# Queries of seven heads by seven block products, the third output block summed in its bank, output rows turned two blocks at a time

## The chip, the cores and the metric

The kernel runs on one core of one Trainium2 chip. The metric is the device time of one execution in microseconds (us). Three runs of the kernel before were timed, and one further execution was profiled. Engine names are those of the profile: PE does matmuls (PEld is its weight load), DVE and ACT are the two elementwise engines, POOL does a few tiny operations, SP issues most transfers. One core means no contention with other cores.

## The reference

Two layers over 528 positions (16 learned ones ahead of 512 tokens) of width 1024, in float32. The first is gated linear attention with four heads; the second is differential attention with eight heads, and this is where two of the three edits lie. Cut to the second layer:

```python
proj = xn @ w_in                       # (528 x 1024) @ (1024 x 8192)
q, k, v, z = jnp.split(proj, 4, axis=-1)          # 2048 columns each: 8 heads x 256
for each head, each block of 128 queries:
    s = einsum('qd,kd->qk', q, k) * 128 ** -0.5 + bias     # two score maps per head
    p = softmax(where(causal, s, -inf))
    a = p[0] - lam * p[1]
    o = head_rms(a @ v) * gnorm * (1 - lambda_init)        # 128 x 256
y = silu(z) * o
out = y @ w_out                                   # (528 x 2048) @ (2048 x 1024)
h = h + out;  final rmsnorm
```

## The kernel before

**Precision.** Every float32 operand is held as a high and a low part (tags ending in h and l, or a pair of tiles): `split` writes the high part by an ACT copy and the low part by a DVE subtraction. A product of two operands is then three matmuls: high by high, high by low, low by high.

**Units.** Most projections of 256 columns are a `Unit`. The 1024 x 256 weights are taken as 2 x 2 blocks of 512 x 128 and the normalised input as 2 x 2 blocks (inner half by token half), and the four output blocks come from seven block products p1 to p7 instead of eight (the Winograd scheme). One product is 12 matmuls (`PASSES`: 4 steps of 128 rows x 3) of 264 columns, or of 256 where only real tokens are wanted (z in the second layer). The scheme needs sums of weight blocks on DVE (`sums` and `outer` in `want_unit`, 4 additions of 128 x 512) and splits of three single blocks (a11, a12, a22: 128 x 512 each) and of two pairs (s21, s43: 128 x 1024 each). The input's own sums are made once per layer.

A unit's bank `bx` runs: p1 is summed in it and copied out by ACT as u1 (`partial`, line 452), p6 is added and copied as u2, p7 is added and copied as u3. The outputs are (0,0) = p1 copy and p2 in bank `by`; (0,1) = u2 and p5 + p3 in bank `bv`; (1,1) = u3 and p5 in `bv`; the third block (1,0) = u3 and p4. In the kernel before, p4 has a bank of its own (`by`, or the second `bx`), and a DVE operation joins it with u3 (line 477). Where a further unit is next in the queue, its p1 is issued between p7 and p4; where none is, p2 or other work stands there. `bx` has two buffers, `by` and `bv` one each.

**Queries.** Head 0's queries, and in the kernel before all heads' queries, are a plain projection (`project`, line 421): two output blocks, each 24 matmuls of 512 columns into one bank, whose result `split` takes from the bank with the scale (lines 279 and 280).

**Order of the work.** The instructions of PE are in program order, which a `Weaver` sets: the attention steps of one head (A scores, B turn the weights, C values, E rows: turn the output, multiply by the gate, split) are issued one after another, and between two steps so many microseconds of queued projection work are filled in (`W.fill`, with an estimated cost per piece). Per head the queue holds z, v, k and q of the next head, in heads 2, 4 and 6 with the output product of two earlier heads ahead of them. k may not start before the last scores of the head are issued (`W.stop`), so k and q stand beside the later steps; before the next head's first scores the queue is worked off and 3.0 us of the following work are filled in. ACT, DVE, POOL and SP are ordered by a scheduler with priorities (`at_once` above `urgent` above `soon`) and run in that order. Weights arrive in `raw` (two buffers) by transfers issued on SP, and are prepared ahead of use as far as buffers allow.

Of the kernel before, what the change touches and what calls it, by code (L numbers as in the profile page):

```python
# [209 lines left out]
def trunk(ctx, tc, x, meta, g_norm, gla_w_in, gla_w_gate_up, gla_b_gate, gla_gnorm, gla_w_out,  # L210
# [225 lines left out]
    class Unit:  # L436
# [26 lines left out]
        def run(self):  # L463
# [4 lines left out]
            nxt = nxt if isinstance(nxt, Unit) else None  # L468
            out = []

            @at_once
            def add(i, n, bank, t, sign):
                if not out:
                    out.extend(o if isinstance(o, list) else [o[:, :self.n], o[:, self.n:]] for o in self.dst())
                o, bank = out[i][n], bank[:, :self.n]
                if sign < 0:
                    W.mark = dve.scalar_tensor_tensor(o, bank, -sc, t, op0=ALU.mult, op1=ALU.subtract)
# [9 lines left out]
                add(0, 0, by, self.p1, 1)  # L487

            def p4():
                bz = pb_tile("by" if nxt else "bx")  # L490
                yield from product(bz, ws.use(a22), X["t4"])
                ws.done(a22)
                add(1, 0, bz, self.u3, -1)
                self.tail(1)

            def p5():
# [937 lines left out]
    def normed():  # L1434
# [11 lines left out]
        spare.update({(2304,): (0, 1, 2), (0, 8, 256): (3,)})  # L1446

# [18 lines left out]
    def want_diff(c):  # L1466
        ws.want_in_order((d_w_in, 0, KT, c), halves_of(P))
# [95 lines left out]
    def tok_tile():  # L1563
        return T(ep, [P, 2 * (256 + NM)], F32, "t", bufs=3)
# [83 lines left out]
        return W.add(gen(), 10.3)  # L1648

    def q_diff_q(hd, s):  # L1650
        want_diff(256 * hd)

        def gen():
            for i in range(2):
                bank = pb_tile("bx" if hd else ("bv", "by")[i])
                yield from project(ws.take(), real2, None, NR, [by_halves(bank)])
                assert not hd or heads[hd - 1].scored
                if i == 0:
                    s.q = [T(ep, [P, 2, NR], F32R, f"q{j}", bufs=1) for j in range(2)]
                urgent(split)(*[t[:, i, :] for t in s.q], bank, scale=-float(P) ** -0.5)  # L1660
        return W.add(gen(), 10.3)

    def diff_steps(hd, s, ys):
# [55 lines left out]
            act.activation(r.on, po, AF.Copy, scale=ms)  # L1719

        @urgent
        def rows(r):
            pt = ps_tile()
            for m in range(2):
                pe.transpose(pt[:, m * P:(m + 1) * P], r.on[:, m * P:(m + 1) * P], ident)  # L1725
            y = T(ep, [P, 2, P], F32, "yt")
            cs = slice(r.ta, r.ta + P)
            W.mark = dve.tensor_tensor(y, pt[:, :256].rearrange("p (m c) -> p m c", m=2), s.z[:, :, cs], op=ALU.mult)
            split(ys[hd][0][:, :, cs], ys[hd][1][:, :, cs], y)

        R = {}
# [1 line left out]
        def A(b):  # L1733
            R[b] = scores(b)

        return A, lambda b: turn(R[b]), lambda b: values(R[b]), lambda b: rows(R[b])

    def want_last(hd):

# [95 lines left out]
    for hd in range(D_HEADS):  # L1835
# [20 lines left out]
        if hd == D_HEADS - 2:  # L1856
# [3 lines left out]
            def freed():  # L1860
# [7 lines left out]
        share = {A: 1.5, B: 1.1, C: 1.1, E: 0.5}  # L1868
        if last:
            steps = steps[:6]  # L1870
        W.fill(3.0)
# [80 lines left out]
```

## Time and profile before

| | |
|---|---|
| median of three runs | 972.04 us (972.03 to 972.95) |
| span of the profiled execution, first to last instruction | 970.2 us, 1.84 us under the median of the runs; the page gives no other time for that execution |
| granted PE clock, mean | 0.999 |
| first layer | to about 480 us |
| scores of the eight heads of the second layer begin at | 500.1, 552.3, 604.9, 678.7, 731.9, 805.3, 858.5, 913.1 us |
| DMA | 104.94 MB, 108 GB/s mean |

In the profile, "xN" is a count, and a group's row gives its busy time, the mean duration of one in ns, and the idle time of its engine just before it with what ended it. Durations of neighbouring instructions overlap, on PE strongly (a matmul's listed duration is two to three times its pace), so the pace of a run of matmuls is read from the start of one group to the start of the next.

### The profile page before, as it was taken

The page shows a single profiled execution, that of the slowest core. Times are in us where ns is not written, and L with a number is a line of the kernel's source. Part 1 is how long each engine was busy: PE and PEld are TensorE (multiplying, and loading weights), DVE is VectorE, ACT ScalarE, POOL GpSimd, SP SyncE. Part 2 cuts the span into 40 slices and gives each one's busy share as a digit, 9 for nine tenths or more (in the row PEclk, how much of TensorE's full clock was granted, in tenths as well). Part 3 has the DMA queues.
Part 4 walks back from the last instruction along what each step waited for, and adds up shares of the span by engine and source line. Part 5 has one row for each costly group of instructions (what it writes and reads, how often), then busy time and mean ns, then how long its engine had stood idle before and what let it go on. Part 6 is the DMA issues. An engine that isn't in the chain of part 4 may idle for free. (4 is left out here: it accounts for less than half of the span.)

```text
span 970.2 us, 18065 instructions
## 1 busy us (share of the span) xinstructions
PE 957.1 (99%) x6993; PEld 906.5 (93%) x6993; DVE 778.4 (80%) x1586; ACT 628.0 (65%) x1304; POOL 50.6 (5%) x68
## 2 busy tenths in 40 slices
PE   8999999999999999999999999999999999999997
PEld 8999999999999999898899998898998999989996
DVE  7989885886888887568997985977958879677785
ACT  7776755577647567656757774576764677655583
POOL 1000000000000100000001001001010000000001
PEclk9999999999999999999999999999999999999999
DMA  7322223635363245224355525135252352412212
GB/s 197 88 86 60 79 81 122 148 99 129 120 156 96 79 121 154 62 92 151 100 132 147 131 78 153 51 97 140 86 148 88 99 138 86 148 61 84 87 66 87
DMA packets 128521, 104.94 MB, mean 108 GB/s; under 512 B 51101, under 2 KB 112829, under 8 KB 128432
## 3 DMA queue, kind: packets, MB, share of 16 engines
q1 hardware_dynamic: 123104, 93.80, 35.1%
q10 hardware_dynamic: 5328, 9.95, 2.8%
q8 instruction: 56, 0.92, 0.4%
q14 instruction: 33, 0.27, 0.1%
HBM read 83.64 MB, written 11.80 MB: 98 GB/s over the span
## 5 line engine op out<-in xcount | busy, mean ns | idle before, releaser
L277 DVE TENSOR_TENSOR wl<-raw,wh 128x1024 fp32r<-128x1024 f32 x98 | 119.5, 1222 | 24.8 <-ACT wh L276 16.8
L276 ACT ACTIVATE wh<-raw 128x1024 fp32r<-128x1024 f32 x98 | 103.2, 1055 | 52.6 <-PE by L968 23.2
L431 PE MATMUL bv<-x,wh 128*128 128x264 f32 (+1 forms) x656 | 97.6, 286 | 0.0
L431 PE MATMUL bx<-x,wh 128*128 128x264 f32 (+1 forms) x640 | 94.9, 286 | 0.7 <-ACT u L452 0.6
L431 PEld LDWEIGHTS bv<-x,wh 128*128 128x128 f32 x656 | 86.5, 188 | 0.6 <-DVE z L479 0.3
L431 PEld LDWEIGHTS bx<-x,wh 128*128 128x128 f32 x640 | 84.5, 188 | 1.9 <-ACT u L452 1.2
L452 ACT ACTIVATE u<-bx 128x264 f32<-128x264 f32 (+1 forms) x120 | 45.4, 380 | 32.3 <-PE bx L431 31.1
L421 PE MATMUL bx<-x,wh 128*128 128x512 f32 (+1 forms) x256 | 62.4, 386 | 0.0
L277 DVE TENSOR_TENSOR wl<-sum,wh 128x1024 fp32r<-128x1024 f32 x41 | 50.1, 1221 | 14.3 <-ACT wh L276 13.9
L431 PE MATMUL bv<-x,wl 128*128 128x264 f32 (+1 forms) x328 | 55.2, 285 | 0.1
L1718 POOL TENSOR_TENSOR st<-st,mhalf 128x1 f32<-128x1 f32 x32 | 31.0, 970 | 464.4 <-ACT on L1716 408.9
L431 PE MATMUL bx<-x,wl 128*128 128x264 f32 (+1 forms) x320 | 53.9, 285 | 0.0
L1682 ACT ACTIVATE p<-p,st 128x528 f32<-128x528 f32 (+3 forms) x64 | 36.5, 571 | 25.4 <-DVE st L1680 24.9
L421 PEld LDWEIGHTS bx<-x,wh 128*128 128x128 f32 x256 | 44.5, 188 | 7.9
L276 ACT ACTIVATE wh<-sum 128x1024 fp32r<-128x1024 f32 x41 | 43.3, 1056 | 13.0 <-PE bv L431 4.0
L431 PE MATMUL by<-x,a12h 128*128 128x264 f32 (+1 forms) x320 | 46.5, 285 | 0.2 <-ACT t L1646 0.2
L431 PE MATMUL bx<-x,a11h 128*128 128x264 f32 (+1 forms) x320 | 46.3, 285 | 0.0
L431 PEld LDWEIGHTS bv<-x,wl 128*128 128x128 f32 x328 | 45.9, 188 | 0.4 <-issue 0.3
L431 PEld LDWEIGHTS bx<-x,wl 128*128 128x128 f32 x320 | 45.2, 188 | 0.6 <-DVE wl L277 0.2
L276 ACT ACTIVATE a11h<-raw 128x512 fp32r<-128x512 f32 x41 | 25.7, 627 | 28.6 <-DMA raw<-in_diff_w_in_dram 14.2
L431 PEld LDWEIGHTS bx<-x,a11h 128*128 128x128 f32 x320 | 42.2, 188 | 0.7
L431 PEld LDWEIGHTS by<-x,a12h 128*128 128x128 f32 x320 | 41.8, 188 | 0.4 <-ACT t L1646 0.4
(475 smaller groups left out, 2632.2 us busy)
## 6 DMA issues: line engine op xcount, KB each, us to landing
raw<-in_gla_w_in_dram SPq DMA_DIRECT2D x48, 512.0 KB, 4.5
raw<-in_diff_w_in_dram SPq DMA_DIRECT2D x42, 512.0 KB, 4.8
raw<-in_diff_w_in_dram SPq DMA_DIRECT2D x11, 1024.0 KB, 6.3
raw<-in_gla_w_out_dram SPq DMA_DIRECT2D x8, 1024.0 KB, 5.7
raw<-in_diff_w_out_dram SPq DMA_DIRECT2D x8, 1024.0 KB, 6.4
vd<-planes ACTq DMA_DIRECT2D x12, 268.0 KB, 7.1
vd<-keep ACTq DMA_DIRECT2D x12, 264.0 KB, 2.3
T<-bdr SPq DMA_DIRECT2D x8, 264.0 KB, 5.0
```

Source lines behind the costliest of these rows:

```text
L276: act.activation(hi, src, AF.Copy)
L277: dve.tensor_tensor(lo, src, hi.bitcast(F32), op=ALU.subtract)
L421: pe.matmul(bank, a[:, k, :], b[k] if n0 is None else b[k][:, n0 + i * nn:n0 + (i + 1) * nn], start=n == 0 and ks[0] == 0, stop=n == len(t ...
L431: pe.matmul(bank[:, :x[q].shape[2]], w[p][:, k * P:(k + 1) * P], x[q][:, k, :], start=first and i == 0, stop=i == len(PASSES) - 1, skip_gr ...
L452: W.moved = act.activation(t, self.bx[:, :self.n], AF.Copy, scale=self.sc)
L1682: act.activation(p[:, :nk], p[:, :nk], AF.Exp, scale=-1.0, bias=st[:, m:m + 1], accum_out=st[:, 2 + m:3 + m])
L1718: pool.tensor_tensor(ms, ms, mhalf[:, :1], op=ALU.pow)
```

## The change

1. **Queries of heads 1 to 7** are a `Unit` over the real tokens (256 columns per matmul), with the scale handed in; its results go to two SBUF tiles (`tok_tile`), and the split takes them from there instead of from the bank. Its cost estimate is 8.9 instead of 10.3 us. The transfer of one 1 MB weight tile becomes two of 512 KB.
2. **In every unit** (20 in the first layer, 21 in the second and the 7 new ones) p4 is added into `bx` after u3 has been copied, and the third block leaves the bank by an ACT copy with scale (`empty`, line 478 after) instead of the DVE operation.
3. **Rows of two blocks at once** in heads 0 to 6: step E is called twice per head instead of four times, with four transposes into one bank, one multiplication of 128 x 512 and one split of that size. Head 7 is as before.

```diff
             def p4():
-                bz = pb_tile("by" if nxt else "bx")
-                yield from product(bz, ws.use(a22), X["t4"])
+                yield from product(self.bx, ws.use(a22), X["t4"], False)
                 ws.done(a22)
-                add(1, 0, bz, self.u3, -1)
+                empty(1, 0)
                 self.tail(1)
+            @at_once
+            def empty(i, n):
+                act.activation(place(i, n), self.bx[:, :self.n], AF.Copy, scale=-sc)
...
     def q_diff_q(hd, s):
-        want_diff(256 * hd)
+        scale, qts = -float(P) ** -0.5, []
...
+        if hd:
+            def dst():
+                tiles()
+                qts.extend([tok_tile()[:, :NR], tok_tile()[:, :NR]])
+                return qts
+            @soon
+            def tail(i):
+                split(*[t[:, i, :] for t in s.q], qts[i])
+            return W.add(Unit(want_unit(d_w_in, 256 * hd), Xr, scale, dst, tail), 8.9)
...
-        def rows(r):
+        def rows(*rs):
+            w = P * len(rs)
             pt = ps_tile()
             for m in range(2):
-                pe.transpose(pt[:, m * P:(m + 1) * P], r.on[:, m * P:(m + 1) * P], ident)
-            y = T(ep, [P, 2, P], F32, "yt")
+                for j, r in enumerate(rs):
+                    pe.transpose(pt[:, m * w + j * P:m * w + (j + 1) * P], r.on[:, m * P:(m + 1) * P], ident)
+            y = T(ep, [P, 2, w], F32, "yt", bufs=1)
...
-        steps = [(A, 0), (A, 1), (B, 0), (A, 2), (C, 0), (B, 1), (E, 0), (A, 3), (C, 1), (B, 2), (E, 1), (C, 2), (B, 3),
-                 (E, 2), (C, 3), (E, 3)]
+        steps = [(A, 0), (A, 1), (B, 0), (A, 2), (C, 0), (B, 1), (A, 3), (C, 1), (B, 2), (E, 1), (C, 2), (B, 3),
+                 (C, 3), (E, 3)]
```

**Where instructions stand now.** The first place is p4 of a z unit in the second layer, on PE. `bx_9865` (before) and `bx_9899` (after) is the next unit's bank, with its p1; the rows that follow are p4. Before:

```order
L431 MATMUL bx_9865<-x_1512_8554,a11h_9736 128x264
L431 MATMUL bx_9865<-x_1513_8555,a11h_9736 128x264
L431 MATMUL bx_9865<-x_1512_8554,a11l_9737 128x264 x4
L431 MATMUL by_9880<-x_1543_8786,a22h_9714 128x256 x8
L431 MATMUL by_9880<-x_1543_8786,a22l_9715 128x256 x4
```

The same place after:

```order
L431 MATMUL bx_9899<-x_1492_8534,a11h_9770 128x264
L431 MATMUL bx_9899<-x_1493_8535,a11h_9770 128x264
L431 MATMUL bx_9899<-x_1492_8534,a11l_9771 128x264 x4
L431 MATMUL bx_9755<-x_1523_8766,a22h_9748 128x256 x8
L431 MATMUL bx_9755<-x_1523_8766,a22l_9749 128x256 x4
```

The products stand in the same order; p4 goes into this unit's own `bx_9755`, which ACT reads as u3 after p7, with one product of 12 matmuls between.

The second place is ACT at the end of head 1, where the queries of head 2 are finished (`q_1835`, after `q_1825`, is the high part of the queries; `wh` a weight pair, `hT` the rows of step E, `on` step C). Before:

```order
L276 ACTIVATE hT_8779<-yt_10343 128x2x128
L279 ACTIVATE q_1835_10360<-bx_10293 128x512
L1715 ACTIVATE ps_10350<-st_10121 128x1
L1716 ACTIVATE on_10355,st_10121<-ps_10350 128x257
L1719 ACTIVATE on_10355<-ps_10350,st_10121 128x256
L276 ACTIVATE wh_10414<-raw_10402 128x1024
L276 ACTIVATE hT_8779<-yt_10383 128x2x128
L279 ACTIVATE q_1835_10360<-bx_10364 128x512
```

The same place after:

```order
L1741 ACTIVATE on_10400<-ps_10395,st_10129 128x256
L452 ACTIVATE u_10426<-bx_10285 128x256
L276 ACTIVATE hT_8759<-yt_10448 128x2x256
L478 ACTIVATE t_10431<-bx_10285 128x256
L276 ACTIVATE q_1825_10428<-t_10431 128x512
L276 ACTIVATE wh_10502<-raw_10490 128x1024
L276 ACTIVATE q_1825_10428<-t_10430 128x512
```

The copy of u3 and the copy of the third block (line 478) are new here, the split reads tiles in SBUF, and one wide `hT` stands for two.

The third place is DVE at the same point: the last operations ahead of head 2's first scores (`wl` is the low part of a weight pair, `yt` step E's multiplication). Before:

```order
L1728 TENSOR_TENSOR yt_10343<-ps_10340,z_9193 128x256
L277 TENSOR_TENSOR wl_10411<-raw_10402,wh_10410 128x1024
L277 TENSOR_TENSOR hT_8779<-yt_10343,hT_8779 128x2x128
L280 SCALAR_TENSOR_TENSOR q_1836_10361<-bx_10293,q_1835_10360 128x512
L1728 TENSOR_TENSOR yt_10383<-ps_10380,z_9193 128x256
L277 TENSOR_TENSOR hT_8779<-yt_10383,hT_8779 128x2x128
L277 TENSOR_TENSOR wl_10415<-raw_10402,wh_10414 128x1024
L280 SCALAR_TENSOR_TENSOR q_1836_10361<-bx_10364,q_1835_10360 128x512
```

The same place after:

```order
L277 TENSOR_TENSOR wl_10499<-raw_10490,wh_10498 128x1024
L484 SCALAR_TENSOR_TENSOR t_10431<-bv_10391,u_10426 128x256
L1752 TENSOR_TENSOR yt_10448<-ps_10443,z_9172 128x512
L488 SCALAR_TENSOR_TENSOR t_10430<-by_10433,u_10307 128x256
L277 TENSOR_TENSOR hT_8759<-yt_10448,hT_8759 128x2x256
L277 TENSOR_TENSOR q_1826_10429<-t_10431,q_1825_10428 128x512
L488 SCALAR_TENSOR_TENSOR t_10430<-bv_10391,u_10389 128x256
L277 TENSOR_TENSOR wl_10503<-raw_10490,wh_10502 128x1024
L277 TENSOR_TENSOR q_1826_10429<-t_10430,q_1825_10428 128x512
```

Behind the last product of the query unit there are now a join (line 488), the ACT copy and the subtraction, where there were the ACT copy and the subtraction, and a `wl` of 1024 columns stands between join and subtraction.

More of the change, by code (lines that the diff above doesn't have):

```diff
@@ L469, in run, with place @@
             out = []
+            def place(i, n):
+                if not out:
+                    out.extend(o if isinstance(o, list) else [o[:, :self.n], o[:, self.n:]] for o in self.dst())
+                return out[i][n]
+            @at_once
+            def empty(i, n):
+                act.activation(place(i, n), self.bx[:, :self.n], AF.Copy, scale=-sc)
             @at_once
             def add(i, n, bank, t, sign):
-                if not out:
-                    out.extend(o if isinstance(o, list) else [o[:, :self.n], o[:, self.n:]] for o in self.dst())
-                o, bank = out[i][n], bank[:, :self.n]
+                o, bank = place(i, n), bank[:, :self.n]
                 if sign < 0:
@@ L1445, in normed @@
             W.defer(2.4 * i, lambda i=i: normed_pair(2 * i))
-        spare.update({(2304,): (0, 1, 2), (0, 8, 256): (3,)})
+        spare.update({(2304,): (0, 1, 2), (256,): (3,)})
     def halved(t):
@@ L1734, in A @@
             R[b] = scores(b)
-        return A, lambda b: turn(R[b]), lambda b: values(R[b]), lambda b: rows(R[b])
+        return A, lambda b: turn(R[b]), lambda b: values(R[b]), lambda b: rows(*([R[b]] if hd == D_HEADS - 1 else [R[b], R[b + 1]]))
     def want_last(hd):
```

17 lines of the change are left out of this document (10 added, 7 removed).

## Prediction

> **What bounds the kernel now.** I read the page's busy shares first, then the heads of the second layer by stage, then PE's timeline where a query projection ends and a unit begins, and last who waits for the copies out of the running bank.
>
> ```profile
> span 970.2 us, 18065 instructions
> PE 957.1 (99%) x6993; PEld 906.5 (93%) x6993; DVE 778.4 (80%) x1586; ACT 628.0 (65%) x1304; POOL 50.6 (5%) x68
> ```
>
> PE is without work for 970.2 - 957.1 = 13.1 us in all. A busy PE is not PE at its peak, though, so what is to be seen next is its pace. Two stretches of the timeline (start, length, engine, line, tiles, shape, count):
>
> ```profile
> 799.85 2.02 PE L421 MATMUL bx<-x,wl 128*128 128x512 f32 x8
> ...
> 801.71 1.11 PE L431 MATMUL bx<-x,a11h 128*128 128x256 f32 x8
> 802.66 0.64 PE L431 MATMUL bx<-x,a11l 128*128 128x256 f32 x4
> 803.13 1.11 PE L431 MATMUL by<-x,a12h 128*128 128x256 f32 x8
> ...
> 805.25 1.64 PE L400 MATMUL ps<-k,q 128*128 128x264 f32 x12
> ...
> 903.26 2.97 PE L421 MATMUL bx<-x,wh 128*128 128x512 f32 x12
> 906.06 0.38 PE L1725 MATMUL ps<-ident,on 128*128 128x128 f32 x2
> ...
> 909.07 1.14 PE L431 MATMUL bx<-x,a11h 128*128 128x264 f32 x8
> ...
> 910.53 1.14 PE L431 MATMUL by<-x,a12h 128*128 128x264 f32 x8
> ```
>
> Start to start: 8 query matmuls of 512 columns take 801.71 - 799.85 = 1.86 us, 0.2325 each (12 of them 2.80 us at 903.26, 0.2333 each). A product of 12 with 256 columns takes 803.13 - 801.71 = 1.42 us, 0.1183 each; one of 12 with 264 columns 910.53 - 909.07 = 1.46 us. The groups follow each other without a gap: the second layer lasts as long as PE's matmuls at their own pace. So an edit is worth what it takes off PE's list, less what it adds in waits.
>
> Whether DVE and ACT have room is read by stage (busy us and count of PE, PEld, DVE, ACT, POOL; then clock and DMA):
>
> ```profile
> 100.00:200.00 100.00, 100.00 (x792) 97.24 (x792) 80.47 (x159) 58.68 (x110) 3.50 (x5) 1.00 0.37 100
> ...
> 552.30:562.00 9.70, 9.70 (x80) 9.69 (x79) 9.60 (x26) 6.77 (x17) 0.00 (x0) 1.00 0.27 91
> 562.00:572.00 10.00, 10.00 (x85) 10.00 (x84) 9.78 (x25) 7.93 (x19) 1.37 (x1) 1.00 0.22 55
> 572.00:582.00 10.00, 10.00 (x85) 9.99 (x84) 6.34 (x19) 8.12 (x19) 0.81 (x1) 1.00 0.41 133
> 582.00:592.00 10.00, 10.00 (x72) 9.27 (x71) 6.64 (x15) 5.74 (x17) 2.02 (x2) 1.00 0.90 190
> 592.00:604.90 12.90, 12.90 (x63) 10.58 (x62) 5.84 (x10) 5.64 (x13) 0.65 (x1) 1.00 0.28 97
> ```
>
> The first row is in the first layer: DVE at 80%, PE never idle. The others are one head. In its first 19.7 us (z, v) DVE is 98% busy and PE does not lose anything, since weights are made ahead. In the last 32.9 us (k, q) DVE is busy 18.82 us and ACT 19.50 us. That is where the queries' extra work goes.
>
> **The queries.** Removed per head: 48 matmuls x 0.2325 = 11.16 us of PE. Added: 7 products of 12, 84 x 0.1183 = 9.94 us. Gain 1.22 us per head, 8.5 us in seven heads. At the 264-column pace (0.1217) it would be 0.94 and 6.6 us, at 0.2333 for the old form 1.26 and 8.8 us; I take 8.5, since z's products have the new ones' shape and operands, and keep 6.6 to 8.8.
>
> What it adds elsewhere has these durations:
>
> ```profile
> L277 DVE TENSOR_TENSOR wl<-raw,wh 128x1024 fp32r<-128x1024 f32 x98 | 119.5, 1222 | 24.8 <-ACT wh L276 16.8 <-PE bx L421 6.0 <-PE bv L431 1.4
> L366 DVE TENSOR_TENSOR sum<-raw 128x512 f32<-128x512 f32 x41 | 28.2, 687 | 7.8 <-DMA raw<-in_gla_w_in_dram 3.8 <-DMA raw<-in_diff_w_in_dram 2.7 <-DVE tick L612 0.9
> L277 DVE TENSOR_TENSOR a11l<-raw,a11h 128x512 fp32r<-128x512 f32 x41 | 28.1, 685 | 3.2 <-ACT a11h L276 2.0 <-PE by L431 1.1
> L280 DVE SCALAR_TENSOR_TENSOR q<-bx,q 128x512 fp32r<-128x512 f32 x14 | 9.6, 684 | 0.1
> L477 DVE SCALAR_TENSOR_TENSOR t<-by,u 128x264 f32<-128x264 f32 x16 | 6.9, 428 | 2.0 <-PE by L431 1.9
> L277 DVE TENSOR_TENSOR hT<-yt,hT 128x256 fp32r<-128x256 f32 x32 | 13.5, 422 | 9.0 <-ACT hT L276 9.0
> L1728 DVE TENSOR_TENSOR yt<-ps,z 128x256 f32<-128x256 f32 x32 | 13.4, 420 | 7.3 <-PE ps L1725 7.3
> ...
> L276 ACT ACTIVATE wh<-raw 128x1024 fp32r<-128x1024 f32 x98 | 103.2, 1055 | 52.6 <-PE by L968 23.2 <-PE bx L421 7.7 <-PE bv L431 6.5
> L276 ACT ACTIVATE a11h<-raw 128x512 fp32r<-128x512 f32 x41 | 25.7, 627 | 28.6 <-DMA raw<-in_diff_w_in_dram 14.2 <-PE bx L431 7.8 <-DMA raw<-in_gla_w_in_dram 5.1
> L276 ACT ACTIVATE hT<-yt 128x256 fp32r<-128x256 f32 x32 | 13.2, 411 | 17.1 <-DVE yt L1728 13.0 <-DVE tick L612 3.7
> L279 ACT ACTIVATE q<-bx 128x512 fp32r<-128x512 f32 x14 | 8.3, 594 | 2.9 <-PE bx L421 2.8
> ```
>
> DVE per head: before 2 x 1.22 + 2 x 0.68 = 3.8 us; after 4 block sums and 3 single blocks of 0.69, 2 pairs of 1.22, 3 joins of 0.43, 2 splits of 0.69, 9.9 us. Added 6.1 us, against 14.1 us free in that head's k and q stage. ACT: before 2 x 1.06 + 2 x 0.59 = 3.3 us; after 3 x 0.63 + 2 x 1.06 + 4 copies of 0.38 (next fence) + 2 x 0.63 = 6.8 us; added 3.5 of 13.4 free. I cost this preparation at nothing, on that cover; if it went, weights would come late by what DVE lacks. On SP, seven 1 MB weight transfers become fourteen of 512 KB. That is seven more issues on SP alone; the queue's order is otherwise as before, the transposing transfer behind the head-1 weights included. Units fetch in this form throughout, and PE's timeline shows none of its groups waiting for it: nothing, at worst a small part of the range.
>
> **The path from the queries to the scores.** Here one thing is on PE's path. The last query matmul ends its turn at 801.71 and the next scores start at 805.25: 3.54 us of z products cover the split. Before, that is ACT 0.59 and DVE 0.68. Now it is a join 0.43, ACT 0.63 and DVE 0.69 = 1.75 us. With one 1.06 us `wh` ahead on ACT and one 1.22 us `wl` on DVE it is 4.03 us, 0.49 over the cover; queued behind it are the next unit's weights, and PE is who waits. So 0 to 3.4 us over seven heads; I take 0.5, one head in which both stand in the way.
>
> **The third block in its bank.** PE's list does not change by it. DVE loses 0.43 us per unit and ACT gains a copy of 0.38; in the first layer, where PE idles nowhere in 100 us, 20 such DVE operations are worth nothing. What is added is a wait: p4 writes the bank that ACT has yet to read as u3, and p3 and the next unit's products are queued behind it on PE. The same hand-off exists twice per unit, p6 after u1 and p7 after u2:
>
> ```profile
> L452 ACT ACTIVATE u<-bx x120: 362/379/396, 88.5 to 930.7; 128x264 f32<-128x264 f32 x99, 128x256 f32<-128x256 f32 x21
> ...
>   PEld bx L431: 1.2, 3
>   PE bx L431: 0.6, 2
> ```
>
> 41 units (the counts of 41 above) make 82 such hand-offs; PE waited in 5 of them, 1.8 us, or 0.022 on average and 0.36 where it waited. Each has one product of some 1.4 us as cover, and p4 has too: the next unit's p1, or p2. New are 48 for p4 and 14 inside the query units, 62 x 0.022 = 1.4 us. Bounds: 0, and 62 x 0.36 = 22 us without cover.
>
> **Rows in pairs.** The 16 transposes per head stay. DVE: 4 x (0.42 + 0.42) = 3.4 us become 2 x (0.69 + 0.69) = 2.7; ACT 4 x 0.41 become 2 x 0.63. Off PE's path, hidden by the fill between values and rows: nothing.
>
> **Sum.** -8.5 + 1.4 + 0.5 = -6.6 us against the span of 970.2, so 963.6. The median of the runs is 1.84 us above that span, so 965.4 us.
>
> **Rivals.**
>
> *Every p4 waits (slower).* If u3's copy came late behind ACT's other work, each unit would lose 0.36 us at p4: 48 x 0.36 = 17.3 us in place of 48 x 0.022 = 1.1, hence 965.4 + 16.2 = 981.6 us. It decides from (8.5 - 0.3 - 0.5) / 48 = 0.16 us per p4 on, and is slower by over 0.2% from 0.20. For it speaks that ACT takes more work; against it the 77 of 82 hand-offs with that cover and no wait, and ACT at 65%. The Trainium skill, page Perfetto Trace Analysis, section Optimizing Tensor Performance (Matmuls), says that independent matmul groups should rotate through different PSUM banks so that evacuation overlaps the next group, and that larger matmuls are more efficient; p4 gives up a bank of its own, so by that rule this is the outcome. The trace agrees so far only in 5 of 82 places.
>
> *The gain is eaten in the second layer.* All seven transitions lose 0.49 us (3.4), and the hand-offs cost double (2.8) as ACT and DVE fill up: -8.5 + 6.2 = -2.3, 969.7 us. For it speaks DVE at 98% in the first part of a head; against it that PE does not lose there.
>
> *Narrow matmuls bring nothing.* If the new products ran at 11.16 / 84 = 0.1329 us per matmul, PE would have the same time as before and the result would be 972 to 974 us. Weight loads are busy 93% already and 252 are added. Against it stands 0.1183, measured in that shape with a weight load per matmul as there will be.
>
> **How the numbers follow.** About 0.2% (1.9 us) is what a measurement of this kernel can tell from no change. Most of the gain arrives (962.3 to 967.5): 0.70. Eaten but for 2 to 4 us (967.5 to 970.1): 0.15. No change, by narrow matmuls or by larger waits: 0.09. Slower by p4's waits: 0.06. So faster 0.85, same 0.09, slower 0.06. The low end is the largest gain, 8.8 us, with no new wait and 0.9 us of the present waits gone (972.04 - 9.7 = 962.3); the high end the smallest gain, 6.6, with 1.4 and 3.4 us of waits (972.04 - 1.8 = 970.2).
>
> **What the profile after would show.** Right: query matmuls of 512 columns only in head 0; 252 matmuls more on PE (7245); products of the query units 1.42 us apart; DVE at 778.4 + 7 x 4.1 (6.1 less 3 x 0.43 and 0.7) - 20 x 0.43 = 799 us, ACT some 37 us up; heads without an output product 1.2 us shorter. Wrong: PE idle ahead of p4 with the u3 copy as releaser, more than a few tenths in all; PE idle at a head's first scores with a query split as releaser; weights as releaser of PE in the k and q stage.

## The result, and the profile after

The changed kernel takes 983.78 us (median of 4 runs, 983.25 to 987.96) against 972.33 us for the kernel before on the same chip: ratio 1.0125, 95% interval 1.0109 to 1.0141. It is some 11.5 us slower, where 6.6 us less were forecast. The profiled execution is the run of 987.96 us, the longest of the four, so its waits are somewhat on the large side.

The page of the kernel after, span and busy times:

```profile
span 986.2 us, 18695 instructions
PE 959.4 (97%) x7245; PEld 920.2 (93%) x7245; DVE 796.7 (81%) x1587; ACT 653.5 (66%) x1380; POOL 43.0 (4%) x68
```

PE's instruction count is the one forecast (7245), and DVE's busy time nearly so (796.7 us for 799). ACT's busy time is up by 25.5 us, where 37 were forecast; added up one by one its instructions take 35.2 us more, but where neighbours overlap, the busy time counts once. PE is idle for 986.2 - 959.4 = 26.8 us, twice the 13.1 of before. The query products have the pace that was forecast; the starts of three in the query unit of head 5, in the timeline:

```profile
804.71 1.11 PE L431 MATMUL bx<-x,wh 128*128 128x256 f32 x8
...
806.12 1.11 PE L431 MATMUL by<-x,a12h 128*128 128x256 f32 x8
...
807.54 1.11 PE L431 MATMUL bx<-x,a22h 128*128 128x256 f32 x8
```

From start to start 1.41 and 1.42 us. So the matmuls bring what they should, and the time is lost between them. Who PE waits for in the second layer (total us, times, longest), before:

```profile
PE bx L431 <- ACT u L452: 0.6, 2, 0.4
PE ps L400 <- DVE yt L1728: 0.2, 1, 0.2
PE by L431 <- ACT t L1646: 0.2, 1, 0.2
```

and after (495 to 986 us):

```profile
PE bv L431 <- DVE t L486: 3.8, 4, 2.0
PE bx L431 <- ACT u L452: 2.1, 3, 1.4
PE ps L400 <- DVE aT L277: 1.3, 3, 0.6
PE ps L1749 <- ACT on L1741: 1.3, 2, 1.1
PE ps L400 <- DVE v L582: 1.1, 1, 1.1
PE ps L400 <- DVE yt L1752: 0.8, 1, 0.8
PE ps L1733 <- DVE am L410: 0.8, 2, 0.5
...
PE ps L400 <- DVE q L277: 0.7, 1, 0.7
PE ps L400 <- ACT v L581: 0.6, 1, 0.6
```

The rows shown hold 12.5 us against 1.0, and they are not one hand-off: joins of units, partial copies, attention weights (`aT`, `am`), rows (`on`, `yt`), values, queries. PE waits for almost everything that ACT and DVE make. Of the prediction's three signs of being wrong one is here, 0.7 us at a head's first scores behind the split of the queries; PE waits 0.3 us in all ahead of a p4, and never for weights. The largest wait in the timeline, in the k and q stage of head 0 (rows of other operations between are left out):

```profile
538.64 0.63 ACT L276 ACTIVATE a11h<-raw 128x512 fp32r<-128x512 f32 x1 [2.80 <-DMA raw<-in_diff_w_in_dram]
539.18 0.37 ACT L452 ACTIVATE u<-bx 128x256 f32<-128x256 f32 x1
539.29 0.65 PE L431 MATMUL bv<-x,wl 128*128 128x264 f32 x4
539.31 0.69 DVE L277 TENSOR_TENSOR a11l<-raw,a11h 128x512 fp32r<-128x512 f32 x1 [1.60 <-ACT a11h L276]
...
541.26 0.70 DVE L366 TENSOR_TENSOR sum<-sum,raw 128x512 f32<-128x512 f32 x1
541.89 0.68 DVE L277 TENSOR_TENSOR a22l<-raw,a22h 128x512 fp32r<-128x512 f32 x1
542.49 0.68 DVE L366 TENSOR_TENSOR raw<-raw 128x512 f32<-128x512 f32 x1
543.09 0.42 DVE L486 TENSOR_TENSOR t<-bv,u 128x264 f32<-128x264 f32 x1
543.56 1.01 PEld L431 LDWEIGHTS bv<-x,wh 128*128 128x128 f32 x8 [2.19 <-DVE t L486]
```

ACT stands 2.80 us for a transfer, splits a block of weights, and DVE, which needs ACT's half first, goes through sums and splits of weights. The last product into `bv` ends about 539.9; the join of it (line 486) starts at 543.09, and the query unit's p5, which needs that bank, 0.47 us later (its weight load waits 2.19 us, PE itself 1.99). Meanwhile both engines have had waits of their own: "busy" is not what was short here, but the turn in the row.

A wait can cost more than its length. The rows of the two stretches around it, before first and then after (PE, PEld, DVE, ACT, POOL with counts; granted clock; DMA):

```profile
545.00:552.00 7.00, 7.00 (x47) 6.24 (x46) 6.96 (x14) 4.59 (x11) 0.55 (x1) 1.00 0.07 17
```

```profile
545.00:552.00 7.00, 6.54 (x31) 6.39 (x30) 3.81 (x8) 3.48 (x9) 1.58 (x1) 0.51 0.48 150
...
886.00:890.00 4.00, 4.00 (x17) 3.48 (x16) 1.30 (x3) 1.12 (x4) 0.55 (x1) 0.57 0.42 148
```

Behind the 2 us wait the granted clock is 0.51 for 7 us, and behind the waits at 884 us 0.57 for 4 us: 7 x 0.49 + 4 x 0.43 = 5.2 us at most, which no row of the waits shows. The four runs were granted 0.991 to 0.997 of full clock on average, the kernel before 0.999. The three runs at 0.994 to 0.997 still took 983.25 to 983.91 us; by these averages, as an estimate, the clock is 2 to 5 us of their loss, and most of it is not the clock.

### The profile page after: what moved, and what is told of

Read it like the earlier page. It is cut to its first block, busy times and chain, and to the rows that moved or that the text cites. A ratio compares the mean times of both kernels' runs of the same rounds, so it can differ in the third digit from the quotient of the medians.

```text
span 986.2 us, 18695 instructions
## 1 busy us (share of the span) xinstructions
PE 959.4 (97%) x7245; PEld 920.2 (93%) x7245; DVE 796.7 (81%) x1587; ACT 653.5 (66%) x1380; POOL 43.0 (4%) x68
## 5 line engine op out<-in xcount | busy, mean ns | idle before, releaser
L431 PE MATMUL bv<-x,wh 128*128 128x264 f32 (+1 forms) x768 | 113.8, 286 | 3.8 <-DVE t L486 3.8
L431 PE MATMUL bx<-x,wh 128*128 128x264 f32 (+1 forms) x752 | 113.1, 288 | 2.3 <-ACT u L452 1.8
L431 PEld LDWEIGHTS bv<-x,wh 128*128 128x128 f32 x768 | 100.8, 189 | 5.0 <-DVE t L486 4.7
L431 PEld LDWEIGHTS bx<-x,wh 128*128 128x128 f32 x752 | 100.1, 190 | 3.7 <-ACT u L452 2.4
L277 DVE TENSOR_TENSOR wl<-sum,wh 128x1024 fp32r<-128x1024 f32 x48 | 58.7, 1224 | 23.7 <-ACT wh L276 22.5
L452 ACT ACTIVATE u<-bx 128x264 f32<-128x264 f32 (+1 forms) x141 | 53.2, 377 | 29.4 <-PE bx L431 29.2
L431 PE MATMUL bx<-x,wl 128*128 128x264 f32 (+1 forms) x376 | 63.4, 286 | 0.0
L431 PE MATMUL bx<-x,a22h 128*128 128x264 f32 (+1 forms) x376 | 55.7, 287 | 0.6 <-ACT u L452 0.3
L431 PE MATMUL by<-x,a12h 128*128 128x264 f32 (+1 forms) x376 | 55.2, 287 | 0.1
L431 PEld LDWEIGHTS bx<-x,wl 128*128 128x128 f32 x376 | 53.2, 190 | 0.2
L431 PEld LDWEIGHTS bx<-x,a22h 128*128 128x128 f32 x376 | 49.2, 189 | 1.3 <-ACT u L452 1.2
L366 DVE TENSOR_TENSOR sum<-raw 128x512 f32<-128x512 f32 x48 | 33.0, 688 | 14.7 <-DMA raw<-in_gla_w_in_dram 7.3
```

The costliest lines, as they stand in the source:

```text
L277: dve.tensor_tensor(lo, src, hi.bitcast(F32), op=ALU.subtract)
L366: dve.tensor_tensor(o, a, b, op=ALU.add)
L431: pe.matmul(bank[:, :x[q].shape[2]], w[p][:, k * P:(k + 1) * P], x[q][:, k, :], start=first and i == 0, stop=i == len(PASSES) - 1, skip_gr ...
L452: W.moved = act.activation(t, self.bx[:, :self.n], AF.Copy, scale=self.sc)
```

## Experiments

Seventeen kernels ran, each beside the kernel before, which took 972.1 to 972.3 us every time. The names of the edits: Q the queries in block products, B the third block summed in its bank, R the rows in pairs. The expectations call PE TensorE, DVE VectorE, ACT ScalarE and POOL GpSimd. Line numbers shift from kernel to kernel: the join of the changed kernel, line 486, is 504 or 479 elsewhere.

| kernel | time, us | ratio to before (95% interval) | DVE / ACT busy, us |
|---|---|---|---|
| before | 972.3 | 1 | 778 / 628 |
| Q | 979.29 | 1.0076 (1.0058 to 1.0094) | 813 / 646 |
| B | 975.78 | 1.0037 (1.0023 to 1.0051) | 766 / 637 |
| R | 974.09 | 1.0019 (1.0007 to 1.0030) | 775 / 624 |
| Q and R | 972.95 | 1.0011 (1.0001 to 1.0021) | 810 / 642 |
| Q and B | 981.16 | 1.0089 (1.0070 to 1.0109) | 797 / 657 |
| Q, B and R (the change) | 983.78 | 1.0125 (1.0109 to 1.0141) | 797 / 654 |

### One edit at a time

Q alone: B and R undone (in `p4` the bank of its own and the DVE join; `rows(r)` and the old steps).

> The kernel before with the query units alone (p4 in its own bank, rows one block at a time, old step order). Theory 1 (hand-offs: 11 us of query matmuls per head that waited for no other engine give way to products that wait for joins and copies every 1.4 us): the 8.5 us that PE saves are lost again to waits ahead of p5, p7 and the first scores of a head, so 972 to 977 us, with a join on DVE or a copy u on ACT as the releaser of PE in 4 us or more. Rival, the bank: the loss comes from p4 behind u3's copy, so without it the queries gain as predicted, 964 to 966 us.

Measured: 979.29 us (977.64 to 981.43). The edit that was to bring 8.5 us, less 0.8 of waits, costs 7 us by itself, more than either expectation has. A join and partial copies hold 4.4 us of PE's waits in the second layer, as theory 1 says, and the 2 us wait at the queries of head 1 is there already (2.10 us at 542.29 us), without the bank.

B alone:

```diff
-                bz = pb_tile("by" if nxt else "bx")
-                yield from product(bz, ws.use(a22), X["t4"])
-                add(1, 0, bz, self.u3, -1)
+                yield from product(self.bx, ws.use(a22), X["t4"], False)
+                empty(1, 0)
```

> The kernel before with p4 summed in the running bank, nothing else. Theory 1: next to no effect, 971 to 974 us, since each p4 has a product of 1.4 us ahead of it. Rival, the bank: 41 p4 that wait 0.25 to 0.36 us each, 982 to 987 us.

Measured: 975.78 us (975.55 to 976.44), between the two ranges expected. What PE waits for most in the second layer:

```profile
PE bx L431 <- ACT u L452: 3.6, 4, 1.4
```

Four waits for a partial copy, up to 1.4 us each, where there were two of at most 0.4. Two of the four stand ahead of a p4 (0.48 and 1.00 us), the others ahead of p6 or p7. Without any block queries this edit is worth +3.5 us.

Two further kernels of that batch were not what their expectations describe: one held Q and R, and the other was B alone once more. Their expectations are given for the record and test nothing.

> The kernel before with rows of two blocks at once and the new order of steps, nothing else. Theory 2 (the third edit takes away the step E that stood between B and C of the last blocks, so the values wait for the turned weights): 975 to 979 us, with PE waiting in the values for aT and am on DVE, 4 to 6 us in seven heads. Prediction: nothing, 972 us.

Measured, as Q and R: 972.95 us (970.55 to 974.47).

> The changed kernel with rows one block at a time and the old order of steps (so edits 1 and 2 together). Theory 2: the third edit's waits go, 976 to 980 us. Theory 1 without theory 2: the third edit has no part, 983 to 984 us. Rival, the bank: 983 to 984 us too.

Measured, as B alone a second time: 975.83 us (974.73 to 976.11), which agrees with 975.78.

The two kernels that were still missing:

```diff
 # the changed kernel, with edit 3 undone
-        def rows(*rs):
+        def rows(r):
-        steps = [..., (B, 1), (A, 3), (C, 1), ..., (B, 3), (C, 3), (E, 3)]
+        steps = [..., (B, 1), (E, 0), (A, 3), (C, 1), ..., (B, 3), (E, 2), (C, 3), (E, 3)]
-        share = {A: 1.5, B: 1.1, C: 1.1, E: 0.7}
+        share = {A: 1.5, B: 1.1, C: 1.1, E: 0.5}
```

> The changed kernel with the output rows turned one block at a time and the steps in the old order: queries in block products and the third block in its bank. Known: queries alone 979.3 us, third block in its bank alone 975.8, all three edits 983.8, kernel before 972.2. Theory A (each edit adds hand-offs of its own, the costs add up, rows in pairs cost nothing): 982.9. Theory B (the bank and the pairs of rows harm each other, since the third product waits for copies that ScalarE makes between the steps): about 979, as queries alone. A time of 983 to 985 says that the rows play no part in the loss.

> The kernel before with the output rows in pairs and the new order of steps, and nothing else. Theory A (hidden by the fill, as the prediction has it): 972.2, within 1 us, and TensorE waits for 'on' or 'yt' no longer than before. Theory B (pairs save TensorE and VectorE stalls, as queries with pairs at 972.95 against queries alone at 979.3 suggests): 966 to 970. Theory C (shorter cover between the turn of the last block and its values): 974 to 976, with waits for aT.

Measured: Q and B 981.16 us (979.52 to 982.97), R 974.09 us (972.48 to 976.96). The first lies between theory A (982.9) and theory B (979) and settles neither; the second lies in the range of theory C, but PE waits nowhere for aT in it. The edits do not add up: R costs 1.9 us alone, saves 6.3 us on top of Q, and costs 2.6 us on top of Q and B; B costs 3.5 us alone, 1.9 us on top of Q and 10.8 us on top of Q and R. No edit has a price of its own here, which suggests that they draw on something that they share.

### What they share: copies on ACT

The third block leaves its bank by DVE in place of ACT; p4 still waits in the bank for u3's copy:

```diff
-                act.activation(place(i, n), self.bx[:, :self.n], AF.Copy, scale=-sc)
+                W.mark = dve.tensor_scalar(place(i, n), self.bx[:, :self.n], -sc, None, op0=ALU.mult)
```

> The changed kernel, in which the third block leaves its bank by one VectorE multiplication into its place in place of one ScalarE copy; the product still waits in its bank for the third partial's copy. Theory A (the loss is that the third product waits in its bank): 982 to 985, and the waits of bx for u stay at 1.4 to 2 us each. Theory B (the loss is that ScalarE's row of work is longer by one copy for every unit, 0.38 us by 42 units, and everything behind it comes later): 975 to 979, with fewer waits for u, am and aT, and VectorE busy 15 us more.

Measured: 973.49 us (971.85 to 977.43), ratio 1.0011 (0.9996 to 1.0025): 10.3 us off the changed kernel. That is below the range of theory B and far from that of theory A. PE's waits of `bx` for partial copies fall from 2.1 to 0.9 us. Its page and the join's wait:

```profile
PE 953.4 (98%) x7245; PEld 915.7 (94%) x7245; DVE 810.2 (83%) x1635; ACT 642.7 (66%) x1332; POOL 44.5 (5%) x68
...
PE bv L431 <- DVE t L486: 2.1, 2, 1.8
```

DVE has 13.5 us more to do and ACT 10.8 us less, and that gives back nine tenths of the loss, although by their shares it is DVE (83%) and not ACT (66%) that is full. With p4 waiting in its bank all the same, the time is 0.5 us from that of Q and R (972.95); so the hand-off in the bank is not the harm in the changed kernel, and the copy on ACT is. One thing goes with it that was not run apart: the edit also renews `W.mark`, the DVE operation behind which a marker for the turned values is set, as the join of the kernel before did. ACT's waits for that marker go from 5.5 to 4.4 us, and a wait of PE at head 6's values (0.62 us at 884.02 us) goes. How much of the 10.3 us is the marker's stays open; by these waits it is the smaller part. That ACT's turn feeds DVE's is seen in DVE's waits in the second layer, kernel before, changed kernel and this one:

```profile
DVE wl L277 <- ACT wh L276: 14.0, 14, 2.4
```

```profile
DVE wl L277 <- ACT wh L276: 23.4, 22, 4.0
```

```profile
DVE wl L277 <- ACT wh L276: 18.4, 18, 2.8
```

Whether the copy harms by where it stands or by its being there:

```diff
-            @at_once
+            @soon
             def empty(i, n):
```

> The changed kernel, with the copy that empties the third block's bank given a lower priority, so that it stands one to a few instructions later in ScalarE's row; its number and length stay. Theory A (the copy does harm by standing ahead of copies and preparations that others wait for): 975 to 980. Theory B (the harm is 0.38 us more of ScalarE's time for each unit, wherever it stands): 982 to 986. Taking it to VectorE gave 973.49.

Measured: 983.78 us (980.92 to 985.35). The edit moves less than its expectation says: in ACT's row only 15 of the 48 copies stand later, by one to four instructions. Such a small shift is worth nothing; a larger one was not tried.

Another instruction of ACT moved to DVE, one that waits for POOL:

```diff
-            act.activation(r.on, po, AF.Copy, scale=ms)
+            dve.tensor_scalar(r.on, po, ms, None, op0=ALU.mult)
```

> The changed kernel, in which the output rows are scaled by their norm (on<-ps,st, 32 times 0.47 us behind GpSimd's power, for which ScalarE stands waiting 19.6 us in the second layer) by VectorE in place of ScalarE. Theory A (ScalarE's row is what is short in the changed kernel: its instructions wait in order, and one taken out of it, with its wait, is worth its length and more): 970 to 978. Theory B (the wait for GpSimd moves to VectorE's row, which is 81% busy and does as much harm there): 982 to 990.

Measured: 977.05 us (976.41 to 981.82), 6.7 us off the changed kernel and in the range of theory A, with DVE at 809.3 and ACT at 642.7 us. The wait for POOL does move to DVE's row (12.6 us), but it does less harm there. Two different instructions moved from ACT to DVE both bring the time down, so ACT's row is what is short in the changed kernel, at 66% busy. Its idle third is largely waiting in order for others. Its largest waits for POOL, for DVE and for transfers in the second layer, before and then after:

```profile
ACT on L1719 <- POOL st L1718: 28.4, 28, 4.1
ACT p L1682 <- DVE st L1680: 24.9, 17, 3.3
...
ACT a11h L276 <- DMA raw<-in_diff_w_in_dram: 14.2, 5, 4.6
```

```profile
ACT p L1704 <- DVE st L1702: 29.7, 19, 3.5
ACT on L1741 <- POOL st L1740: 19.6, 25, 1.7
ACT a11h L276 <- DMA raw<-in_diff_w_in_dram: 18.5, 6, 4.6
```

They come to 67.5 us before and 67.8 after, so the change did not add them: they were there, and were no room. What it added is work between them, and with it DVE's waits for ACT shown above.

### The preparation and the hand-offs of the queries

The query units read tiles that lie ready; the transfer, splits and sums of their weights are left out (so is the split of the weights, 2.4 us of DVE and 2.1 of ACT per head, that the kernel before needed for its form):

```diff
-            return W.add(Unit(want_unit(d_w_in, 256 * hd), Xr, scale, dst, tail), 8.9)
+            return W.add(Unit(want_bare(), Xr, scale, dst, tail), 8.9)      # parts: tiles of X["b11"]
```

> The changed kernel, in which the block products of the queries of heads 1 to 7 read tiles of the normed input that lie ready, in place of weights of their own: the transfer, the splits and the block sums of these weights are left out, every product, partial copy and join of the queries stays. Theory A (ScalarE and VectorE have too much preparation of weights in their rows, and the copies and joins for which TensorE waits stand behind it): 960 to 968. Theory B (the added hand-offs themselves, three copies and four joins for a head, are what TensorE waits for): 976 to 983, waits of bx for u and of bv for t as in the changed kernel.

Measured: 969.02 us (968.66 to 970.38), 14.8 us off the changed kernel and 1 us above the range of theory A:

```profile
PE 950.7 (98%) x7245; PEld 914.4 (94%) x7245; DVE 755.8 (78%) x1524; ACT 631.0 (65%) x1345; POOL 41.1 (4%) x68
...
PE bv L449 <- DVE t L504: 1.2, 2, 0.7
...
PE bx L449 <- ACT u L470: 0.7, 2, 0.4
```

Every hand-off is still there, and the joins and copies wait a third as long. Some 5 us stay between this and 964.1 us, which PE's shorter list alone would give (972.3 - 8.2, worked out further down). Transfers, ACT's work and DVE's work are left out together here, so the run doesn't tell them apart.

The hand-offs taken away in place of the preparation (no copies of the query units' partial sums, which are missing from the output):

```diff
-            self.p1 = self.partial()
+            self.p1 = None if self.plain else self.partial()        # u2 and u3 likewise
...
+                if self.plain:
+                    W.mark = dve.tensor_scalar(o, bank, sc, None, op0=ALU.mult)
```

> The changed kernel, in which the query units make no copies of their partial sums: the seven products of a head are issued as before, and each of the four output blocks leaves its bank by one VectorE multiplication (the partial sums are left out of the output); weights, transfers, splits and sums of the queries stay. ScalarE has 3 copies of 0.37 us less for a head. Theory A (preparation): 978 to 984. Theory B (the hand-offs): 966 to 972, and the waits of bx for u in the 256-column products go.

Measured: 981.16 us (979.03 to 983.09), in the range of theory A. The hand-offs inside the query units, with their 21 copies on ACT, are worth 2.6 us, their preparation up to 14.8. The two numbers overlap with the 10.3 us of the copy: together they are more than was lost.

### Order in the rows

The weights that stood ahead of the join at 543 us, put behind the queries' last join (for heads 2, 4 and 6):

```diff
+    def after_joins(on):                    # ACT behind W.moved, DVE behind W.mark
...
-                with tc.issue_after(W.moved.ins) if calm and b == 0 else ExitStack():
+                with tc.issue_after(W.moved.ins) if calm and b == 0 else after_joins(later and b == 0):
```

> The changed kernel, in which the first weight block and the sums for the gate projection of heads 2, 4 and 6 are prepared behind the last join of the queries of the head before, on ScalarE and on VectorE; everything is computed as before. Theory A (that preparation, which waits for a late transfer, stands ahead of the joins of keys and queries in the two engines' rows, and TensorE waits for the joins): 975 to 979; the wait of bv for the join at 543.6 us (2.0 us) and those at 674.3 and 686.4 us go, and with them the stretch of half clock behind 545 us. Theory B (the waits come from the number of hand-offs, not from what stands ahead of them): 983 to 985, the waits of bv and bx stay or move. A time above 986 would say that the gate's own weights come late in turn.

Measured: 985.56 us (985.33 to 985.96), just above the range of theory B. The wait for the join goes from 3.8 to 0.7 us, and others come:

```profile
PE bx L439 <- ACT wh L276: 5.0, 4, 1.4
PE by L439 <- DVE a12l L277: 2.0, 2, 1.0
```

What was taken from the joins was missing at the weights. The same on Q and R, with the preparation behind the keys' last join only:

> Queries in block products and output rows in pairs, without the third block in its bank (972.95 us in an earlier run), and the first weights and the sums for the gate projection of heads 2, 4 and 6 are prepared behind the keys' last join, before the queries' joins. Theory A (the join of keys at about 544 us, for which TensorE waits 2.0 us, stands behind that preparation, which itself waits for a transfer): the wait goes, and 969 to 971.5. Theory B (the two engines have no room in that stage, and the wait comes back at the next user of these weights, as with the preparation behind the queries' joins, 985.56 against 983.78): 972 to 974.5.

Measured: 977.14 us (975.42 to 978.65), 4.2 us slower than Q and R as it was and above both ranges; PE's wait for the join at 544 us grew from 1.8 to 3.1 us. These two changes of order bring nothing; both expectations that they would (theory A each time) were wrong.

### Where in the second layer

Lengths of the stretches from the first scores of one head to those of the next (the last one to the end), in us, from the timelines:

| kernel | 0 | 1 | 2 | 3 | 4 | 5 | 6 | 7 |
|---|---|---|---|---|---|---|---|---|
| before | 52.2 | 52.6 | 73.8 | 53.2 | 73.4 | 53.3 | 54.6 | 57.1 |
| the change | 58.0 | 53.1 | 75.2 | 54.1 | 72.6 | 54.5 | 59.5 | 58.3 |
| Q and R | 55.9 | 52.9 | 72.0 | 51.4 | 72.4 | 51.9 | 57.8 | 55.9 |
| third block by DVE | 57.9 | 52.8 | 72.0 | 51.4 | 72.3 | 52.0 | 57.7 | 57.6 |
| heads 2 to 6 | 53.1 | 52.8 | 72.0 | 52.5 | 72.1 | 52.5 | 60.0 | 57.8 |
| heads 2 to 7 | 55.4 | 52.9 | 72.0 | 52.5 | 72.1 | 52.5 | 57.7 | 55.7 |
| heads 2 to 7, values earlier | 55.2 | 52.8 | 72.0 | 52.5 | 72.1 | 52.5 | 55.5 | 55.7 |

With Q and R and no copy of the third block on ACT, heads 2 to 5 give 1.0 to 1.8 us each, about as forecast (1.2); heads 0 and 6 lose 3 to 6 us. With Q alone, heads 4 and 5 were longer than before (75.5 and 54.3 us). So Q was tried for fewer heads, with R and without B:

```diff
-        if hd:
+        if 1 < hd < D_HEADS - 1:          # second kernel: if hd > 1
```

> Queries in block products for heads 2 to 6 alone (heads 1 and 7 by the plain projection as before), output rows in pairs, the third block not in its bank. With seven heads so the time was 972.95 us; there the stretch from the first scores of head 0 to those of head 1 was 55.9 us against 52.2 before and that of head 6 57.8 against 54.6, while those of heads 2 to 5 were shorter by 1.0 to 1.8 us each. Theory A (the loss sits in the two stages that prepare heads 1 and 7, where the other work for VectorE is largest; elsewhere the products bring what was predicted): 964 to 968. Theory B (every head's preparation costs about as much as its products bring, and the stages share the loss by chance): 970 to 973.

> Queries in block products for heads 2 to 7, head 1 plain, output rows in pairs, third block not in its bank. Seven heads so: 972.95 us; heads 2 to 6 alone: 976.57, where the stretch of head 6 (from its first scores to those of head 7) was 60.0 us against 57.8 with seven, and the stretch of head 0 53.1 against 55.9. If the plain projection of head 7 made head 6 longer there, this gives 53 us for head 0, 57 to 58 us for head 6, and 970 to 973. If the stretches share the time by chance, head 6 is at 59 to 60 again and the time 974 to 977.

Measured: heads 2 to 6 976.57 us (974.86 to 976.70), heads 2 to 7 970.62 us (969.97 to 974.52). The first is above both ranges; the second is in its range of 970 to 973, but with 55.4 us for head 0 where 53 were expected. The theory of the two stages was half wrong: with head 7 plain, head 6 is longer in the profile, not shorter. And the head-0 stretches, 53.1 and 55.4, belong to two kernels that are alike up to there. The difference begins at POOL: its tiny power in step C, then ACT's scaling and the attention weights behind it, heads 2 to 7 (rows of other operations left out here and in the next view):

```profile
540.89 3.23 POOL L1734 TENSOR_TENSOR st<-st,mhalf 128x1 f32<-128x1 f32 x1 [10.47 <-ACT on L1732]
541.29 1.22 DVE L277 TENSOR_TENSOR wl<-raw,wh 128x1024 fp32r<-128x1024 f32 x1
542.42 0.68 DVE L366 TENSOR_TENSOR raw<-raw,sum 128x512 f32<-128x512 f32 x1
543.03 0.68 DVE L277 TENSOR_TENSOR a22l<-raw,a22h 128x512 fp32r<-128x512 f32 x1
544.15 0.47 ACT L1735 ACTIVATE on<-ps,st 128x256 f32<-128x256 f32 x1 [3.34 <-POOL st L1734]
544.52 0.27 ACT L276 ACTIVATE aT<-ps 128x128 fp32r<-128x128 f32 x1
...
544.84 0.71 PE L400 MATMUL ps<-v,aT 128*128 128x256 f32 x3 [1.40 <-ACT aT L276]
```

and heads 2 to 6, where the same operation took 0.85 us:

```profile
540.09 0.85 POOL L1734 TENSOR_TENSOR st<-st,mhalf 128x1 f32<-128x1 f32 x1 [9.32 <-ACT on L1732]
540.53 1.21 DVE L277 TENSOR_TENSOR wl<-raw,wh 128x1024 fp32r<-128x1024 f32 x1
540.98 0.47 ACT L1735 ACTIVATE on<-ps,st 128x256 f32<-128x256 f32 x1 [0.96 <-POOL st L1734]
```

A difference of 2 us in one stretch of one profile is thus within chance, and the table should be read with that, head 6's 60.0 and 57.7 us too. The times of the two kernels, 6 us apart, do not overlap.

Head 6's own loss: PE waits 1.1 us there for the split values. Moving that split some ten DVE instructions ahead (`0.0 if odd else 5.0 if head 6 else 11.0` in `turned_back2`):

> As the kernel with heads 2 to 7 in block products, with head 6's values split some ten VectorE instructions earlier, ahead of the sums and splits of the next weights. In all kernels with block queries in head 6 TensorE waits 1.1 to 1.4 us for these values at 872 to 885 us, and its next products run at half clock. Theory A (the wait is one of order in VectorE's row): the wait goes, head 6 is 2 to 3 us shorter and the time 2 to 4 us under that of the other kernel. Theory B (the stage is full, and the wait comes back behind the next weights): within 1 us of it.

Measured: 970.15 us (968.36 to 972.20), ratio 0.9975 (0.9964 to 0.9986). The row below, in the kernel without the move, is gone, and head 6 takes 55.5 in place of 57.7 us:

```profile
PE ps L400 <- DVE v L576: 1.1, 1, 1.1
```

Between the two kernels the medians differ by 0.5 us with overlapping runs, so the 2 to 4 us of theory A did not come, and the gain of the move is seen in the stretch and not settled in the time. The half clock that the expectation gives behind this wait stands in 4 of the 12 traces that have the wait, each time with another of 0.56 to 0.63 us just ahead of it. With the rows scaled by DVE as well:

> The kernel with heads 2 to 7 in block products, rows in pairs and head 6's values split earlier (970.15 us), with the rows scaled by VectorE as well. Theory A: 963 to 968, and the wait for aT at 544.7 us (1.56 us), which stands behind that scaling on ScalarE, goes. Theory B: 972 to 978.

Measured: 970.21 us (968.97 to 973.49), ratio 0.9978 (0.9966 to 0.9989): no further gain, and between the two ranges. PE's wait for ACT's aT goes, and waits for DVE's aT (1.9 us) and for the rows that DVE now scales (1.8 us) stand in its place. So where no copy of the third block is on ACT, ACT's row is no longer alone in being short. Both kernels are 2.1 us faster than the kernel before, and 13.6 faster than the changed one.

## Why the prediction was wrong

*Queries, -8.5 us: right on PE's list.* By the median from start to start in the kernel before, 588 matmuls more of 256 columns (0.118 us each) and 336 fewer of 512 (0.231) come to 69.4 - 77.6 = -8.2 us. The rival that narrow matmuls bring nothing is refuted by 1.41 us per product, and heads 2 to 5 in Q and R are shorter by about what was forecast.

*"I cost this preparation at nothing, on that cover": this is the step that failed.* The cover was 14.1 us of DVE and 13.4 us of ACT, totals over one head's k and q stage. Free time on an engine that runs in order is cover only if it falls ahead of the instruction that is waited for. In that stage of the kernel before (572 to 604.9 us) ACT's free time was its own waiting, 5.5 us for POOL, 3.3 for PE and 2.5 for DVE, and DVE's was such too, 7.5 us for ACT and 4.1 for PE. What is put in behind such a wait starts late itself and pushes on what follows, as at 543 us. Taking the preparation away gives 14.8 us, an upper bound, since that kernel also lacks what the old form had.

*The third block in its bank, "worth nothing" but for a hand-off: the same step.* The prediction let DVE lose and ACT gain and weighed neither, and took the first layer, where PE idles nowhere, for all. The copy is worth 10.3 us in the changed kernel, shown by moving it to DVE. The whole edit costs 3.5 us by itself; there the copy was not moved, and part is the hand-off (p4 waits 1.5 us).

*Hand-offs, +1.4 us: mis-sized, and at the wrong place.* 0.022 us each was read too large and was an average over a kernel with room. The five waits are three hand-offs, since PE and its weight load wait for the same copy at 677.84 and 682.81 us, and PE itself lost 0.55 us in 82, 0.007 each. In the changed kernel the waits of `bx` for u and of `bv` for joins are 5.9 us in the second layer. But p4 is not where they fall: of the three waits for u one is at a p4 (0.29 us, at 535.90 us); the longest, 1.42 us at 686.41 us, and those for joins are at other products. So the rival "every p4 waits", whose 981.6 us is nearest to the result, named another mechanism, and with p4 waiting in its bank all the same the DVE version takes 973.49 us. The nearness is luck. The rule weighed there, of the Trainium skill, page Perfetto Trace Analysis, section Optimizing Tensor Performance (Matmuls), that independent matmul groups should rotate through different banks, is borne out in part only: the bank alone costs 3.5 us, but in the changed kernel it costs nothing once DVE empties it.

*Queries to scores, +0.5 us:* 0.7 us in one wait (`ps` for q). Right.

*Rows in pairs, nothing:* +1.9 us alone, -6.3 us with Q, +2.6 us with Q and B. Wrong as a constant; with Q it takes instructions from both rows (ACT -4, DVE -3 us), which would fit the above, but with Q and B it takes 3 us from ACT and is slower. Why stays open.

*Not in the sum at all:* the clock. Some 5 us of the profiled execution are lost at half clock behind waits of about 2 us.

What stays open: how the shared loss divides among transfers, ACT and DVE; the single effects (14.8, 10.3, 2.6) overlap and were measured one at a time. Whether a plain head 7 lengthens head 6 (by 2 us in one profile) wasn't followed up. Whether a third buffer for `raw` would take away waits for transfers wasn't tried.

## What to carry to other kernels

Busy shares of in-order engines are no cover: before counting added elementwise work as free, find the instruction that PE waits for next and what stands ahead of it in its row, and count that engine's own waits as occupied. When two engines split one operation (ACT the high part, DVE the low), the one with the lower busy share can be the short one; moving an instruction across is one run that tells which. Price edits that load the same engines together, and allow for the half clock that may follow each new PE wait of about 2 us (1.7 or 3.4 us where it came here).

## What the hardware showed that was not expected

- **Half clock behind short waits.** A wait of 2.0 us at 543.56 us, with some tenths around it, was followed by 7 us at a granted 0.51. In the kernel with Q and R a wait of 1.8 us at the same place had no such stretch (granted 1.00 from 546 to 556 us), and one of 3.1 us, in Q and R with its weights prepared later, had none either. Where such a stretch came in the second layer of these traces, ahead of the last 20 us, it was 3.4 us long, and 6.8 us in the one case above. The Trainium skill, page TensorE: Matmul & The Clock Gate, section HAM oscillation, warns of idle gaps beyond about 3.4 us; the trace shows the drop at shorter ones, not each time.
- **A short POOL operation of very uneven length.** The 128x1 power, 0.57 us in the median of its line in the kernel with heads 2 to 7, took 3.23 us there while DVE ran additions and subtractions of two tiles back to back, and ended where they paused (544.12 us, with DVE's last end at 543.71); ACT and PE stood behind it. The Trainium skill, page SBUF — State Buffer, section two separate sides, says that a DVE operation with two SBUF inputs and a GpSimd operation that reads SBUF exclude each other on a shared pair of ports, whichever starts first keeping it. The rows above agree with it, but do not show it: in the kernel with heads 2 to 6 the same power took 0.85 us and ended in the midst of such a subtraction. It is not what the change cost: the 32 powers of the second layer take 31.0 us in the kernel before and 23.5 in the changed one.
